# Starting the staging tiles, all slots and the memory's keys at a multiple of 128 bytes

## The chip, the cores and the metric

The kernel runs on one core of a Trainium2 chip. The metric is the device time of one execution in microseconds (us); the time before is the median of three runs. Trace and profile come from one more execution, with the hardware profiler on.

## The reference

One layer of a streaming encoder, all in float32: batch 1, 1024 tokens, width 1024, 256 memory tokens.

```python
h = x
mem_n = rmsnorm(mem, norm_mem_w)
h = h + head_group_mixer(rmsnorm(h, norm_mix_w), ...)           # conv of 31 taps || retention, 8 heads
h = h + memory_cross_attention(rmsnorm(h, norm_xattn_w), mem_n, xq_w, xkv_w, xo_w)   # 4 heads of 256
h = h + sq_relu_mlp(rmsnorm(h, norm_mlp_w), mlp_up_w, mlp_down_w)    # square(relu(h @ up)) @ down, 4096 wide
out = rmsnorm(h, norm_f_w)
```

The mixer projects h to 512 + 512 conv channels, 256 queries, 256 keys, 512 values and 512 gates; one half goes through a gated depthwise convolution, LayerNorm and silu, the other through chunked retention with rotary phases and a GroupNorm; both meet in `w_out`.

## The kernel before, in words

**Products in three parts.** TensorE takes float32 in two formats. Plain float32 serves the transposes and the small products of retention. All large products run in the format fp32r, and to keep precision each operand is split in two tiles, `hi` (rounded to fp32r by ScalarE, line 110) and `lo` (the rest, by VectorE, line 111). `mm3` then issues three matmuls into one PSUM bank: hi x hi (line 128), hi x lo (line 129), lo x hi (line 130). Of each matmul one operand is stationary (128 x 128, loaded ahead by LDWEIGHTS) and one moves through (128 x 512, or 128 x 256 for the memory's projections and the attention scores). In the profile's rows the moving operand is named first, the stationary one second.

**Where tiles lie.** On-chip memory is given out by pools, in bytes of each partition; every tile's size is rounded up to 32 bytes. From the left: `keep` (the identity with the rotary frequencies, 576 bytes; `mhalf`, 8 columns of -0.5 for the power -0.5 in `rstd_of`; `junk`, 4096; `par`, 560), then `raws` (three staging tiles `raw` of 4096, into which weights are loaded), `small` (the `tiny` statistics) and `slots`: 39 tiles `s0` to `s38` of 4096 bytes each. Nearly everything passes through these slots: a free list (`get`, `put`) hands them out and takes them back. The left pools begin at byte 16,512, behind what the runtime and four constants keep.

From the right end of the memory, at byte 229,344, pools come and go by stage: `ra` for retention's small tiles (`qb`, `st`, `rot`, `kT`, ...), `rw` for the residual rows, `rx` for the attention's keys `kT_hi` and `kT_lo` (8192 bytes each), and `rm`, eight more slots `r0` to `r7` for the MLP, which join the free list. When the MLP begins, the three staging tiles join it too.

**Stages in order.** Norm and transposes of memory and x, with the memory's projections in between (0 to 110 us); conv inputs, gates and values, with the 31 taps of each of four channel groups as 124 products on VectorE (line 433; 100 to 295 us); retention and the output projection (to 520 us); cross-attention, and the norm for the MLP (to 690 us); the MLP (690 to 1314 us). The MLP is done as two levels of 2 x 2 blocks with seven products instead of eight, so VectorE also forms sums of weights and of activations (line 907), and results are spilled to DRAM (`a`) and read back.

The order of instructions on each engine is made by the framework's scheduler from its own time model of the program. All DMAs are issued from SP's queue.

Of the kernel before, what the change touches and what calls it, by code (L numbers as in the profile page):

```python
# [7 lines left out]
F32 = mybir.dt.float32  # L8
# [6 lines left out]
P = 128  # L15
# [53 lines left out]
def encoder_layer(ctx: ExitStack, tc: tile.TileContext, x, mem, positions, norm_mix_w, w_in, conv_w, conv_b,  # L69
# [10 lines left out]
    keep = ctx.enter_context(tc.tile_pool(name="keep", bufs=1))  # L80
# [52 lines left out]
    ident_if = keep.tile([P, C_DM], F32, name="ident_if")  # L133
    sync.dma_start(ident_if[:], consts[:, :C_DM])
    ident, invf = ident_if[:, :P], ident_if[:, C_IF:C_DM]
    mhalf = keep.tile([P, 8], F32, name="mhalf")
    vec.memset(mhalf[:], -0.5)

    def rstd_of(ss, n, scale, cols=1):
# [144 lines left out]
    right = ctx.enter_context(ExitStack())  # L284
# [351 lines left out]
    right = ctx.enter_context(ExitStack())  # L636
# [44 lines left out]


    right = ctx.enter_context(ExitStack())
    rx = right.enter_context(tc.tile_pool(name="rx", bufs=1, side="right"))
    kT_hi = rx.tile([P, 8, M], F32R, name="kT_hi")
    kT_lo = rx.tile([P, 8, M], F32R, name="kT_lo")
# [95 lines left out]

    rm = ctx.enter_context(tc.tile_pool(name="rm", bufs=1, side="right"))
    slots.extend(rm, [f"r{i}" for i in range(8)])
    urow = row(norm_mlp_w)
# [413 lines left out]
def build(nc, arrays_of):  # L1201
    args = []
    for name, a in arrays_of:
        args.append(nc.dram_tensor(f"in_{name}_dram", a.shape, mybir.dt.from_np(a.dtype), kind="ExternalInput").ap())
    args.append(nc.dram_tensor("out_0_dram", (1, S, D), F32, kind="ExternalOutput").ap())
    with tile.TileContext(nc, schedule_with_timeline_sim=True) as tc:
        encoder_layer(tc, *args)
# [12 lines left out]
```

## Time and profile before

| | |
|---|---|
| time, median of 3 runs | 1316.72 us (1315.59 to 1317.78) |
| the profiled execution, and its span | 1315.49 us, 1313.7 us |
| TensorE busy, matmuls | 1281.3 us (98%), 6093 |
| VectorE busy | 862.2 us (66%) |
| ScalarE busy | 549.3 us (42%) |
| GpSimd busy | 95.7 us (7%) |
| mean granted TensorE clock | 0.998 of full |
| DMA | 167 MB, queue busy 36.7% of 16 engines |

Matmuls are pipelined: the duration of one in the rows (about 0.39 us for 512 columns) includes its way through the array, while the next one starts some 0.23 us after it. What counts for the pace is the interval between starts, which the timeline gives. A float32 product in the plain format is run as two passes and shows as two matmuls.

### The profile page before, as it was taken

What the parts mean: (1) busy time and instruction counts of PE and PEld (TensorE: products, weight loads), DVE (VectorE), ACT (ScalarE), POOL (GpSimd) and SP (SyncE); (2) the same over time, 40 slices, a digit from 0 to 9 for tenths busy, and PEclk for the clock granted to TensorE, in tenths of its full rate; (3) what the DMA queues carried; (4) which work ended last, traced back from release to release, by engine and by line L of the source; (5) the groups of instructions that cost most, each with busy time, mean ns of one, the idle gap of its engine ahead of it and who ended that gap; (6) DMA issues with size and microseconds to landing.
All of it is one profiled execution on the core that took longest, in us unless ns stands there. A gap on an engine that the chain in (4) does not pass through costs nothing.

```text
span 1313.7 us, 15796 instructions
## 1 busy us (share of the span) xinstructions
PE 1281.3 (98%) x6093; PEld 1061.6 (81%) x6093; DVE 862.2 (66%) x1090; ACT 549.3 (42%) x1015; POOL 95.7 (7%) x157
## 2 busy tenths in 40 slices
PE   6999999999999999999998999999999999999997
PEld 5898887877888888888876888888888888888886
DVE  6676999987756424574568565465565976567744
ACT  7533112155845323452236455444455344323422
POOL 3192000011211000000000000000000000000002
PEclk9999999999999999999999999999999999999999
DMA  9552103312132301322142444333479544444213
GB/s 343 161 155 88 32 17 96 112 41 89 45 132 100 125 0 42 102 98 81 53 140 80 176 176 160 138 103 145 160 272 402 186 148 144 151 147 151 96 64 128
DMA packets 82099, 166.99 MB, mean 127 GB/s; under 512 B 5309, under 2 KB 42309, under 8 KB 82024
## 3 DMA queue, kind: packets, MB, share of 16 engines
q1 hardware_dynamic: 82024, 165.98, 36.7%
q8 instruction: 48, 0.79, 0.2%
q14 instruction: 27, 0.22, 0.1%
HBM read 119.83 MB, written 46.14 MB: 126 GB/s over the span
## 4 chain that ended last, share of the span: by engine, by line
PE 80%; DVE 10%; DMA 4%; POOL 3%; issue 2%; ACT 1%; SPq 0%; POOLq 0%; ACTq 0%; DVEq 0%
PE mm L130 21%; PE mm L129 21%; PE mm L128 21%; DVE s L433 6%; PE tp L129 4%; PE tp L128 4%; PE tp L130 3%; POOL s L328 2%; DVE s L111 2%; POOL s L333 1%; PE mm L516 1%; PE mm L532 1%; DMA s<-in_x_dram 1%; DMA raw<-in_w_out_dram 1%; DMA kvT_d<-s 1%
## 5 line engine op out<-in xcount | busy, mean ns | idle before, releaser
L129 PE MATMUL mm<-s,s 128*128 128x512 f32 (+1 forms) x1298 | 493.6, 381 | 3.9 <-DVE s L111 2.4
L128 PE MATMUL mm<-s,s 128*128 128x512 f32 (+1 forms) x1272 | 484.6, 383 | 3.3 <-ACT s L852 1.0
L130 PE MATMUL mm<-s,s 128*128 128x512 f32 (+1 forms) x1222 | 461.1, 380 | 2.4 <-DVE s L111 2.4
L129 PEld LDWEIGHTS mm<-s,s 128*128 128x128 f32 x1298 | 244.2, 188 | 50.4 <-DVE s L111 3.2
L128 PEld LDWEIGHTS mm<-s,s 128*128 128x128 f32 x1272 | 239.3, 188 | 49.2 <-DVE s L771 1.4
L130 PEld LDWEIGHTS mm<-s,s 128*128 128x128 f32 x1222 | 229.8, 188 | 45.7 <-DVE s L111 3.0
L110 ACT CAST s<-s 128x1024 fp32r<-128x1024 f32 x101 | 104.7, 1050 | 140.7 <-DVE s L907 38.6
L433 DVE SCALAR_TENSOR_TENSOR s<-s,par,s 128x1009 f32<-128x1009 f32 (+25 forms) x120 | 146.2, 1286 | 0.5
L111 DVE TENSOR_TENSOR s<-s,s 128x1024 fp32r<-128x1024 f32 x81 | 98.3, 1223 | 54.6 <-ACT s L110 42.0
L111 DVE TENSOR_TENSOR s<-raw,s 128x1024 fp32r<-128x1024 f32 x64 | 79.1, 1242 | 57.5 <-ACT s L110 23.8
L110 ACT CAST s<-raw 128x1024 fp32r<-128x1024 f32 x66 | 69.2, 1053 | 94.6 <-PE mm L129 15.3
L142 POOL TENSOR_SCALAR tiny<-tiny 128x1 f32<-128x1 f32 (+1 forms) x50 | 17.9, 359 | 1180.2 <-ACT junk L160 925.5
L907 DVE TENSOR_TENSOR s<-s,s 128x1024 f32<-128x1024 f32 x38 | 45.9, 1222 | 7.4 <-DMA s<-in_mlp_down_w_dram 5.3
L129 PE MATMUL mm<-s,r 128*128 128x512 f32 x124 | 48.8, 394 | 0.0
L128 PE MATMUL tp<-s,s 128*128 128x512 f32 x120 | 47.0, 391 | 0.0
L110 ACT CAST s<-r 128x1024 fp32r<-128x1024 f32 x26 | 27.1, 1048 | 42.5 <-PE mm L129 13.5
L130 PE MATMUL tp<-s,s 128*128 128x512 f32 x114 | 44.3, 390 | 0.0
L162 DVE SCALAR_TENSOR_TENSOR s<-s,tiny,s 128x1024 f32<-128x1024 f32 x23 | 29.4, 1283 | 20.2 <-POOL tiny L143 12.8
L111 DVE TENSOR_TENSOR s<-r,s 128x1024 fp32r<-128x1024 f32 x22 | 26.8, 1224 | 22.1 <-ACT s L110 15.5
L130 PE MATMUL mm<-s,r 128*128 128x512 f32 x100 | 39.4, 394 | 0.0
L160 ACT ACTIVATE junk<-s 128x1024 f32<-128x1024 f32 x24 | 25.5, 1064 | 32.8 <-DVE s L1111 24.5
L130 PE MATMUL mm<-r,s 128*128 128x512 f32 x98 | 38.5, 393 | 0.0
(273 smaller groups left out, 1856.1 us busy)
## 6 DMA issues: line engine op xcount, KB each, us to landing
s<-in_mlp_down_w_dram SPq DMA_DIRECT2D x24, 512.0 KB, 3.8
s<-in_mlp_up_w_dram SPq DMA_DIRECT2D x23, 512.0 KB, 4.2
aS<-s SPq DMA_DIRECT2D x22, 512.0 KB, 8.1
raw<-in_w_in_dram SPq DMA_DIRECT2D x20, 512.0 KB, 4.2
s<-aS SPq DMA_DIRECT2D x20, 512.0 KB, 3.3
s<-a SPq DMA_DIRECT2D x19, 512.0 KB, 4.5
a<-s SPq DMA_DIRECT2D x18, 512.0 KB, 2.8
raw<-in_xkv_w_dram SPq DMA_DIRECT2D x16, 512.0 KB, 4.4
```

What stands on the lines that cost most here:

```text
L110: act.copy(hi[:], raw[:])
L111: vec.tensor_tensor(out=lo[:], in0=raw[:], in1=f32(hi[:]), op=ALU.subtract)
L128: pe.matmul(ps, lh, rh, start=first, stop=False, skip_group_check=goes_on)
L129: pe.matmul(ps, lh, rl, start=False, stop=False, skip_group_check=goes_on)
L130: pe.matmul(ps, ll, rh, start=False, stop=last, skip_group_check=goes_on)
L142: pool.tensor_scalar(out=v[:], in0=ss, scalar1=scale, scalar2=EPS, op0=ALU.mult, op1=ALU.add)
L160: act.activation(junk[:], src, AF.Square, accum_out=ss[:])
L162: vec.scalar_tensor_tensor(out=dst, in0=src, scalar=rs[:], in1=r, op0=ALU.mult, op1=ALU.mult)
L328: pool.tensor_scalar(out=o, in0=i, scalar1=a, scalar2=None, op0=op0)
L333: pool.tensor_tensor(out=o, in0=a, in1=b, op=op)
L433: vec.scalar_tensor_tensor(out=accs[m][:, s:], in0=us[m][:, :S - s], scalar=cw(m, k), in1=accs[m][:, s:], op0=ALU.mult, op1=ALU.add)
L907: vec.tensor_tensor(out=o[:], in0=a[:], in1=b[:], op=ALU.subtract)
```

## The change

`mhalf` becomes 32 columns wide (128 bytes instead of 32), which moves everything allocated behind it on the left up by 96 bytes. On the right, a tile of 24 columns (96 bytes) that nobody writes or reads is allocated ahead of the keys' pool `rx` and of the MLP's pool `rm`, which moves their tiles down by 96 bytes. The pools `ra` and `rw` stay where they were.

```diff
-    mhalf = keep.tile([P, 8], F32, name="mhalf")
+    mhalf = keep.tile([P, 32], F32, name="mhalf")
     vec.memset(mhalf[:], -0.5)
...
     right = ctx.enter_context(ExitStack())
+    gap = right.enter_context(tc.tile_pool(name="gapx", bufs=1, side="right"))
+    gap.tile([P, 24], F32, name="rx_gap")
     rx = right.enter_context(tc.tile_pool(name="rx", bufs=1, side="right"))
     kT_hi = rx.tile([P, 8, M], F32R, name="kT_hi")
     kT_lo = rx.tile([P, 8, M], F32R, name="kT_lo")
...
+    gap = ctx.enter_context(tc.tile_pool(name="gap", bufs=1, side="right"))
+    gap.tile([P, 24], F32, name="rm_gap")
     rm = ctx.enter_context(tc.tile_pool(name="rm", bufs=1, side="right"))
     slots.extend(rm, [f"r{i}" for i in range(8)])
```

## The prediction

> **What bounds the kernel now.** I read the page first, then busy time by stretch, then the groups of matmuls by shape, then the timeline of TensorE at six places.
>
> ```profile
> span 1313.7 us, 15796 instructions
> PE 1281.3 (98%) x6093; PEld 1061.6 (81%) x6093; DVE 862.2 (66%) x1090; ACT 549.3 (42%) x1015; POOL 95.7 (7%) x157
> PEclk9999999999999999999999999999999999999999
> PE 80%; DVE 10%; DMA 4%; POOL 3%; issue 2%; ACT 1%; SPq 0%; POOLq 0%; ACTq 0%; DVEq 0%
> ```
>
> TensorE is busy 98% of the span at full granted clock, and 80% of the chain that ended last is TensorE. A change pays here only if it shortens the interval from one matmul to the next, or an idle stretch of TensorE, of which there are 1313.7 - 1281.3 = 32 us. The stretches say where that holds:
>
> ```profile
> core 0: us, PE busy (x) PEld busy (x) DVE busy (x) ACT busy (x) POOL busy (x), PEclk, DMA share, GB/s
> 100.00:295.00 195.00, 190.81 (x853) 155.87 (x852) 177.24 (x184) 49.15 (x118) 10.25 (x18) 1.00 0.21 65
> 295.00:690.00 395.00, 391.88 (x1995) 326.52 (x1994) 223.65 (x431) 170.65 (x499) 29.99 (x60) 1.00 0.25 84
> 690.00:1290.00 600.00, 596.43 (x2593) 487.30 (x2592) 383.74 (x383) 270.90 (x301) 6.17 (x8) 1.00 0.45 161
> ```
>
> In the MLP (690 to 1290 us) VectorE is busy 64% and ScalarE 45%; TensorE alone sets the pace, with 596.4/2593 = 230.0 ns a matmul. In the convolution (100 to 295) VectorE is at 177.2 of 195, so a faster TensorE meets a second bound there after 17.8 us.
>
> **What one matmul costs, and where its operands start.** The starts are not in the trace; they follow from the order and sizes of the tiles. The left pools begin at byte 16,512 = 129 x 128. Ahead of the staging stand 576 + 32 + 4096 + 576 = 5280 = 41 x 128 + 32 bytes, then come 3 x 4096 of staging and 1024 of small tiles: every staging tile and every slot `s` starts 32 bytes past a multiple of 128, and so do all their slices, which are cut at multiples of 512. The right end lies at 229,344 = 1791 x 128 + 96, so the eight slots `r` and the keys start 96 past. No fp32r operand of the kernel starts at a multiple of 128. First both operands at 32 (operands print moving first, stationary second; of each run the first and the last row):
>
> ```profile
> 149.80 0.39 PE L129 MATMUL mm<-s,s 128*128 128x512 f32 x1
> 151.84 0.39 PE L129 MATMUL mm<-s,s 128*128 128x512 f32 x1
> 15.06 0.28 PE L130 MATMUL mm<-s,s 128*128 128x256 f32 x1
> 20.34 0.28 PE L129 MATMUL mm<-s,s 128*128 128x256 f32 x1
> ```
>
> Ten 512-wide matmuls, nine steps: 2.04/9 = 226.7 ns. Forty-five 256-wide ones, 44 steps: 5.28/44 = 120.0 ns. The difference is 106.7 ns for 256 columns, 0.417 ns each, so 512 columns stream in 213.4 ns and 13.3 ns a matmul is something else, the same at both widths: as long as 32 columns, which are 128 bytes of a row. Now plain float32, which the trace runs at half that rate, its operands just as far from a multiple of 128 (96 in `qb`, 32 in `s`):
>
> ```profile
> 301.45 0.59 PE L516 MATMUL mm<-qb,kT 128*128 128x512 f32 x1
> 302.74 0.59 PE L516 MATMUL mm<-qb,kT 128*128 128x512 f32 x1
> 303.17 0.38 PE L524 MATMUL mm<-s,kz 128*128 128x256 f32 x1
> 303.38 0.59 PE L524 MATMUL mm<-s,kz 128*128 128x256 f32 x2
> ```
>
> The first pair is the first and last of four, three steps of 430 ns; the 256-wide take 210 to 220. That is twice the column time and next to nothing beside it: loading a new stationary block costs no 13 ns when the moving operand comes at half rate. The 13.3 ns belongs to reading at full rate. Whether it belongs to the start address, other starts can say:
>
> ```profile
> 1002.76 0.39 PE L128 MATMUL mm<-r,s 128*128 128x512 f32 x1
> 1008.13 0.40 PE L130 MATMUL mm<-r,s 128*128 128x512 f32 x1
> 626.06 0.39 PE L128 MATMUL mm<-s,r 128*128 128x512 f32 x1
> 629.27 0.39 PE L130 MATMUL mm<-s,r 128*128 128x512 f32 x1
> 469.59 0.28 PE L129 MATMUL mm<-kT_lo,s 128*128 128x256 f32 x1
> 470.73 0.28 PE L130 MATMUL mm<-kT_hi,s 128*128 128x256 f32 x1
> ```
>
> Moving at 96, stationary at 32: 24 matmuls, 5.37/23 = 233.5 ns. Moving at 32, stationary at 96: 15 matmuls, 3.21/14 = 229.3 ns. The keys, at 96 and 256 wide: 1.14/10 = 114 ns against 120 at 32. So the interval does hang on where operands start, to a finer or coarser grain than 32 bytes, and not in one direction. No row shows a start at 0; that is the unknown of this change.
>
> **The change, part by part.**
> 1. `mhalf` grows from 8 to 32 columns: staging and all slots `s` move up by 96 bytes, to 21,888 = 171 x 128 and 35,200 = 275 x 128. The gaps on the right move the keys to 212,864 and `r` to 196,480, both multiples of 128. No instruction, DMA or wait is added; the gap tiles are never written. The memset of `mhalf` writes 24 more columns:
>
> ```profile
> L137 DVE MEMSET mhalf<- x1: 65/65/65, 0.8 to 0.8; 128x8 f32 x1
> 1.64 4.51 DMA s<-in_mem_dram
> ```
>
> At VectorE's 1 ns a column or so it goes from 65 to about 90 ns, at 0.8 us, while everything waits for the first load until 6.1 us. Hidden; without that cover 0.03 us.
>
> 2. The interval of the fp32r matmuls. Its price at start 0 is bounded by rows: 213.4 ns (columns alone) from below, 233.5 ns (the dearest start shown) from above. I take 216: the float32 row that streams for the same time, 256 columns at double time, steps at 210 to 220, and it is the nearest row in which TensorE reads without being short of data. The reason for the lower end: the excess is one 128-byte piece at both widths, what a row of 2048 or 1024 bytes costs when it straddles one piece more than it fills (17 instead of 16, 9 instead of 8); from a multiple of 128 it straddles none.
>
> The loops give 4896 fp32r matmuls 512 wide: 2688 in the MLP (8 x 7 x 2 x 4 x 3 up, 2 x 7 x 4 x 4 x 2 x 3 down), 2208 before. MLP: 2688 x (230.0 - 216) = 37.6 us. Before it: 2208 x (226.7 - 216) = 23.6 us. The 576 matmuls 256 wide could give 10 ns each, 5.8 us; but TensorE then also loads a 128-wide block each 109 ns, as the transposes' pace shows:
>
> ```profile
> 20.58 1.47 PE L170 MATMUL tp<-ident_if,s 128*128 128x128 f32 x12
> L170 PE MATMUL tp<-ident_if,s x128: 270/272/273, 20.6 to 468.1; 128*128 128x128 f32 x128
> ```
>
> (1.47 - 0.27)/11 = 109 ns a step. And most of those 576 lie before 110 us among loads and the angle chain. I count 2 of 5.8. Sum before losses: 37.6 + 23.6 + 2 = 63 us.
>
> 3. What is late next. Convolution: some 770 such matmuls give 8.2 us there, out of 17.8 us that VectorE has idle, and its products run back to back:
>
> ```profile
> 174.25 30.83 DVE s L433 x27
> L433 DVE SCALAR_TENSOR_TENSOR s<-s,par,s 128x1009 f32<-128x1009 f32 (+25 forms) x120 | 146.2, 1286 | 0.5
> ```
>
> I give back half, 4 us. Between 295 and 690 us retention, norms and softmax hand over among three engines; of 1995 matmuls' gain I give back 3 us. MLP: splits at 1.05 us on ScalarE and 1.22 on VectorE keep their lead at 64% and 45% busy (68% and 48% after); its DMA share rises from 0.45 to 0.48. I give back 2 us. Sum 63 - 9 = 54 us.
>
> The profiled execution took 1315.5 us (span 1313.7 and 1.8 around it); the median of the runs is 1316.7, 1.2 more. 1315.5 - 54 = 1261.5, as a median 1262.7.
>
> 4. VectorE, ScalarE and DMA read and write the same tiles. The convolution's products already start at every multiple of 4 bytes:
>
> ```profile
> L433 DVE SCALAR_TENSOR_TENSOR s<-s,par,s 128x999 f32<-128x999 f32 x4 | 5.1, 1277 | 0.0
> L433 DVE SCALAR_TENSOR_TENSOR s<-s,par,s 128x1000 f32<-128x1000 f32 x4 | 5.1, 1276 | 0.0
> L433 DVE SCALAR_TENSOR_TENSOR s<-s,par,s 128x1002 f32<-128x1002 f32 x4 | 5.1, 1276 | 0.0
> ```
>
> The output of 1000 columns starts 24 columns in, at 32 + 96 = 128, so at a multiple of 128; its neighbours 4 and 8 bytes away: 1276 to 1277 ns. Nothing for VectorE. For the other two I take nothing: they carry 1% and 4% of the chain, 13 and 53 us, and and a twentieth of these, about the share that the excess has of a matmul, is 0.7 and 2.7 us to either side, within the range below.
>
> [...]
>
> **The rivals.**
> - *Only the mixing goes* (0.27). The excess comes from moving and stationary reads meeting, which hangs on their difference; at 32/32 it is 226.7 and at 0/0 the same. For: the start of the stationary operand shifts the interval too (229.3). Against: the rest is 32 columns to the digit. MLP 2688 x (230.0 - 226.7) = 8.9 us, little elsewhere: about 1308. If the excess falls only in part, to 223 ns (16 columns cheaper from 96 to 32, 8 more from 32 to 0 in proportion to the bytes), 2688 x 7 + 2208 x 3.7 = 27 us: 1290.
> - *Start 0 is a dear one* (0.12), the one on the other side. The keys at 96 are cheaper than 32, `r` at 96 dearer, so the order isn't known. If at 0 both reads begin on the same piece and each matmul takes 233.5 ns, 2688 x 3.5 + 2208 x 6.8 = 24 us slower: 1341. It decides from an interval above some 228.5 ns, the present mean (230.0 MLP, 226.7 before).
> - *The change does nothing* (0.08): no grain that matters, 1316.7; as would a gain that VectorE takes back everywhere, against which stands its 64% in the MLP.
>
> **The numbers.** Forecast, start 0 costs 216 ns: 0.53, with its own range 1250 to 1285 (213.4 ns without losses is 2688 x 16.6 + 2208 x 13.3 = 74 us, 1243; double losses give 1272, 219 ns at that some 1286). The range of 8 in 10 takes in the second case too: 1250 to 1310. A measurement tells 0.2% (2.6 us) from no change. Faster by more: 0.53 + 0.27 = 0.80; within: 0.08; slower: 0.12.
>
> **What would show it.** Steps of 216 ns in the 512-wide runs, the same for `s`, `r` and staging; about 600/217 = 2760 matmuls in 600 us of MLP where 2593 stood; VectorE over 93% in the convolution, with new idle time of TensorE there; float32 steps unchanged at 430 and 215. Wrong if the steps stay at 226.7, or all take one value above 228.5, or if a different order of instructions moves the time more than the steps do (the longer memset enters the scheduler's own time model).

## The result, and the profile after

| | before | changed |
|---|---|---|
| median of 6 runs each | 1317.25 us | 1309.47 us |
| ratio of the changed kernel to before | | 0.9946 (0.9934 to 0.9959) |
| profiled execution, its span | 1315.5 us, 1313.7 us | 1311.6 us, 1309.8 us |

By the medians the change gains 7.8 us (0.59%), by the ratio 0.54%, which is 7.1 us. A gain of 54 us was forecast. It is the first rival, "only the mixing goes", that came out, with its 1308 us. The profiled execution of the changed kernel lies 2.1 us above its median: apart from the very end of the span its granted clock drops to one half in three spells, 13.7 us in all, where the profiled execution before has one spell of 3.4 us. The 512-wide fp32r matmuls that fall into these spells step at 427 ns, which adds 4.2 us to the changed kernel and 1.6 us to the one before. That is one reason why its span shows only half of the gain, 3.9 us; the intervals between matmuls show it better. All ratios in this document leave out two disturbed executions, one of the kernel before (4427 us) and one of e6 (1610 us).

First the page after, with lines that the prediction shows of the page before:

```profile
span 1309.8 us, 15796 instructions
PE 1279.6 (98%) x6093; PEld 1066.4 (81%) x6093; DVE 862.3 (66%) x1090; ACT 548.4 (42%) x1015; POOL 95.7 (7%) x157
PE 78%; DVE 13%; POOL 3%; DMA 3%; issue 2%; ACT 1%; SPq 0%; POOLq 0%; ACTq 0%; DVEq 0%
```

The instructions are the same, each engine is busy for about the same time, and TensorE is still the bound. Busy time by stretch (columns as in the prediction):

```profile
100.00:295.00 195.00, 191.21 (x850) 156.15 (x849) 177.19 (x183) 48.88 (x117) 9.22 (x16) 0.99 0.21 65
295.00:690.00 395.00, 392.10 (x1984) 326.76 (x1983) 223.23 (x430) 169.21 (x497) 29.98 (x60) 1.00 0.26 84
690.00:1290.00 600.00, 596.35 (x2621) 492.73 (x2620) 385.73 (x387) 273.25 (x305) 6.91 (x10) 0.99 0.46 162
```

In the MLP (the last row) 2621 matmuls stand where 2593 stood. That is 596.35/2621 = 227.5 ns a matmul instead of 230.0, and 2688 x 2.5 ns = 6.7 us of the 7.8. The prediction showed a run of 24 matmuls in which `r` moves against `s`; its first and last row are now:

```profile
1002.62 0.39 PE L128 MATMUL mm<-r,s 128*128 128x512 f32 x1
1007.83 0.39 PE L130 MATMUL mm<-r,s 128*128 128x512 f32 x1
```

5.21/23 = 226.5 ns instead of 233.5. But `s` with `s`, now at a multiple of 128 each, has not become faster in itself: in the convolution (100 to 295 us), where both operands lie in `s` throughout, the mean interval of the 512-wide ones is 226.9 ns before and after. Over the whole trace, taking every two 512-wide fp32r matmuls that follow each other within 250 ns, the intervals average 227.1 ns (before 228.6), and 4299 of 4712 are 226 or 227 ns, where 2971 of 4725 were before. The commonest interval is what it was; what went are the longer ones.

### The profile page after: what moved, and what is told of

Read it like the earlier page. It is cut to its first block, busy times and chain, and to the rows that moved or that the text cites. A ratio compares the mean times of both kernels' runs of the same rounds, so it can differ in the third digit from the quotient of the medians.

```text
span 1309.8 us, 15796 instructions
## 1 busy us (share of the span) xinstructions
PE 1279.6 (98%) x6093; PEld 1066.4 (81%) x6093; DVE 862.3 (66%) x1090; ACT 548.4 (42%) x1015; POOL 95.7 (7%) x157
## 4 chain that ended last, share of the span: by engine, by line
PE 78%; DVE 13%; POOL 3%; DMA 3%; issue 2%; ACT 1%; SPq 0%; POOLq 0%; ACTq 0%; DVEq 0%
PE mm L130 21%; PE mm L129 21%; PE mm L128 21%; DVE s L433 9%; PE tp L128 3%; PE tp L130 3%; PE tp L129 3%; DVE s L111 2%; POOL s L328 2%; PE mm L516 1%; POOL s L333 1%; PE mm L532 1%; ACT s L110 1%; DMA raw<-in_w_out_dram 1%; DMA s<-in_conv_w_dram 1%
## 5 line engine op out<-in xcount | busy, mean ns | idle before, releaser
L130 PEld LDWEIGHTS mm<-s,s 128*128 128x128 f32 x1222 | 230.9, 189 | 43.8 <-DVE s L111 1.7
L433 DVE SCALAR_TENSOR_TENSOR s<-s,par,s 128x1009 f32<-128x1009 f32 (+25 forms) x120 | 146.1, 1276 | 0.5
```

Source lines behind the costliest of these rows:

```text
L130: pe.matmul(ps, ll, rh, start=False, stop=last, skip_group_check=goes_on)
L433: vec.scalar_tensor_tensor(out=accs[m][:, s:], in0=us[m][:, :S - s], scalar=cw(m, k), in1=accs[m][:, s:], op0=ALU.mult, op1=ALU.add)
```

## The experiments

There were two theories at first. S: a start at a multiple of 128 pays by itself. D: what counts is how the starts of moving and stationary operand differ. Theory S is the forecast cut down to what the profile had shown.

**Halves of the change, and equal starts at 32.** Either half alone, and a version in which everything starts 32 past a multiple of 128 (the edits in short, against the kernel before):

```diff
 e1_left_only     mhalf 8 -> 32 columns, no gaps
 e2_all_at_32     mhalf 8, both gaps   gap.tile([P, 16], ...)     # 64 bytes
 e3_right_only    mhalf 8, both gaps   gap.tile([P, 24], ...)     # 96 bytes
```

> Only the left half of the change: staging and slots s start at 0 past a multiple of 128, the slots r and the keys stay at 96. Theory D (the interval hangs on the difference between the starts of moving and stationary operand, modulo 128; equal starts give 226.7 ns wherever they lie): s with s steps at 226.7 as before, and runs that mix s and r keep an excess, as the difference is now 96 instead of 64; so the time lies between 0.9946 and 1.003 of before, most likely 0.997 to 1.000. Theory S (a start at a multiple of 128 is what pays, and the profile of the changed kernel shows all that it pays): most fp32r matmuls have both operands in s, so most of the gain comes here, 0.995 to 0.997, and s with s steps differ from those of before.

> The left side as before (32 past a multiple of 128), on the right gaps of 64 bytes, so that r and the keys start at 32 too: all starts alike, none at a multiple of 128. Theory D: the same as the whole change, 0.9935 to 0.996 of before (1309 to 1311 us), mean interval of the 512-wide fp32r matmuls 227.1 ns as there. Theory S: no better than before, 0.998 to 1.002, as nothing starts at a multiple of 128.

> Only the right half: r and the keys at a multiple of 128, staging and slots s at 32 past one. Theory D: the mixed runs have a difference of 32 instead of 64; no gain as with equal starts, 0.996 to 1.003. Theory S: the runs in which r moves (455 matmuls) step at 226.7, a gain of about 2 us, 0.998 to 0.999.

Measured, as ratio to before with the 95% interval: left half 1.0015 (1.0006 to 1.0024), right half 1.0010 (1.0000 to 1.0020), all at 32 0.9999 (0.9990 to 1.0008). Neither half gains, so S falls: most matmuls have both operands in `s`, which the left half alone puts at a multiple of 128. But D modulo 128 falls too: with all starts at 32, the MLP has the old pace.

```profile
690.00:1290.00 600.00, 596.46 (x2593) 488.12 (x2592) 382.49 (x384) 272.08 (x303) 4.52 (x7) 0.99 0.45 160
```

(Busy time by stretch, all starts at 32: 2593 matmuls, as before the change.) What the theory overlooked: in that kernel `s` lies at 288 and `r` at 416 past a multiple of 512, alike modulo 128 and 128 apart modulo 256; in the changed kernel both lie at 384.

**The matmul alone.** A kernel that leaves out the layer and has runs of 48 matmuls, here the loop of one run:

```python
for i in range(REP):      # REP is 48; m, s: first columns of moving and stationary operand, set per run
    a = s + (i % 8) * 128
    b = m + (i % 2) * 512
    pe.matmul(ps[:rows, :cols], st[:, a:a + rows], mv[:, b:b + cols], start=i == 0, stop=i == REP - 1)
```

> The layer is left out; the output is a copy of rows of x. On TensorE stand runs of 48 fp32r matmuls, each with a stationary block of its own (eight in turn) and one of two moving halves, with the starts set: 0/0, 32/32, 64/64, 64/0, 0/64, 96/32, 32/96, 32/0, 0/32, 4/4, 4/0, 96/0, 16/0, 0/96 (moving/stationary, bytes past a multiple of 128); at 0/0 also stationary blocks of 64 and of 32 columns, moving operands of 384 and of 256 columns, and bfloat16. Theory D: 226.7 ns at 0/0, 32/32, 64/64 and 4/4, more (about 233) at differences of 64. Theory S: 0/0 is below 32/32 and 64/64. What the 13.3 ns beyond 512 columns are: if it is the loading of the stationary block that takes reads from the moving operand (theory L), blocks of 64 columns step at about 220 ns and of 32 at about 217, and bfloat16, with half the bytes, at about 216; if it is a fixed cost of each fp32r matmul (theory F), 226.7 for 64 and 32 columns too, and 173.3 for 384 moving columns under both.

In its timeline each run is one row, start and length first. A row ends with its last matmul, so (length - 0.39)/47 is the mean interval of a 512-wide run:

```profile
19.29 11.36 PE L53 MATMUL bboth<-mov,sta 128*128 128x512 f32 x48
41.65 11.36 PE L53 MATMUL dmov<-mov,sta 128*128 128x512 f32 x48
52.84 11.17 PE L53 MATMUL esta<-mov,sta 128*128 128x512 f32 x48
119.83 11.68 PE L53 MATMUL kmovfour<-mov,sta 128*128 128x512 f32 x48
131.35 11.26 PE L53 MATMUL lhalf<-mov,sta 128*64 128x512 f32 x48
142.45 11.23 PE L53 MATMUL mquart<-mov,sta 128*32 128x512 f32 x48
201.25 11.32 PE L53 MATMUL pagain<-mov,sta 128*128 128x512 f32 x48
```

In order, moving/stationary: 32/32 gives 233.4 ns, 64/0 233.4, 0/64 229.4, 4/0 240.2, then 0/0 with stationary blocks of 64 and of 32 columns 231.3 and 230.6, and 0/0 with full blocks 232.6. No 512-wide fp32r run reached 226.7, a miss of both theories as they stood. The short blocks miss both explanations of the 13.3 ns: theory L had them at 220 and 217, theory F at 226.7. The two tiles lay 128 apart modulo 512 here, so equal starts modulo 128 were a difference of 128. That made the theory D256 (or D512): moving and stationary operand must start alike modulo 256 (or 512).

**Deciding on the layer.** Three kernels that differ from the kernel before or from the changed one by the gaps alone, and the change once more (the edits in short):

```diff
 e5_equal_not_128   mhalf 8,  gap.tile([P, 48], ...)   # s, r, keys at 288 modulo 512: alike, none at a multiple of 128
 e6_128_not_equal   mhalf 32, gap.tile([P, 56], ...)   # all at multiples of 128; s at 384, r and keys at 256 modulo 512
 e7_equal_mod_256   mhalf 8,  gap.tile([P, 112], ...)  # s at 288, r and keys at 32 modulo 512
```

> The left side as before, on the right gaps of 192 bytes: staging, slots s, slots r and keys all start at 288 past a multiple of 512, none at a multiple of 128. In the changed kernel all start at 384 past a multiple of 512; in the one with all starts at 32 past a multiple of 128, r lies at 416 and s at 288 past a multiple of 512, which differs by 128. Theory D256/D512 (what counts is that moving and stationary operand start alike modulo 256, or 512): the same gain as the whole change, 0.9935 to 0.996, 512-wide steps 227.1 ns on average. Theory S (multiples of 128): none, 0.998 to 1.002.

> The changed kernel with 128 bytes more in both gaps on the right: every start is a multiple of 128, but r and the keys lie at 256 and s at 384 past a multiple of 512. Theory D256/D512: the gain is gone, 0.998 to 1.002, and r moving against s steps at 231 to 234 ns. Theory S: the gain stays, 0.9935 to 0.996.

> The left side as before, gaps of 448 bytes on the right: s at 288, r and the keys at 32 past a multiple of 512; alike modulo 256, not modulo 512. D256: the gain as in the changed kernel, 0.9935 to 0.996. D512: no gain, 0.998 to 1.002. Theory S: no gain.

> The changed kernel once more beside these on the same chip, for the comparison: 0.993 to 0.996 under every theory.

| | ratio to before | 95% interval |
|---|---|---|
| alike, none at a multiple of 128 (e5) | 0.9943 | 0.9929 to 0.9958 |
| all at multiples of 128, not alike (e6) | 0.9998 | 0.9987 to 1.0010 |
| alike modulo 256 only (e7) | 0.9954 | 0.9940 to 0.9969 |
| the change again (e8) | 0.9942 | 0.9928 to 0.9956 |

The whole gain comes without a single start at a multiple of 128, and with every start at one it is gone. The rows of the MLP for e5, e6 and e7, in this order:

```profile
690.00:1290.00 600.00, 596.36 (x2617) 492.81 (x2616) 385.88 (x387) 272.91 (x304) 6.91 (x10) 0.99 0.46 162
```

```profile
690.00:1290.00 600.00, 596.46 (x2593) 488.02 (x2592) 382.31 (x383) 272.40 (x304) 3.84 (x6) 0.99 0.45 160
```

```profile
690.00:1290.00 600.00, 596.35 (x2622) 492.89 (x2621) 386.50 (x386) 272.82 (x305) 6.66 (x10) 1.00 0.46 163
```

2617, 2593 and 2622 matmuls. In e6 the run of 24 with `r` moving:

```profile
1006.25 0.40 PE L128 MATMUL mm<-r,s 128*128 128x512 f32 x1
1011.62 0.39 PE L130 MATMUL mm<-r,s 128*128 128x512 f32 x1
```

5.37/23 = 233.5 ns, as before the change, from a multiple of 128.

**By difference, alone.** The kernel of e4 with the two tiles alike modulo 512, and moving minus stationary set per run:

> The layer is left out, the output is a copy of rows of x; again runs of 48 fp32r matmuls alone, now by the difference of the starts (moving minus stationary). In the first such kernel the two tiles lay 128 apart modulo 512, so that its runs had differences of 128 (steps 232 to 233 ns), 64 (228.9), 192 (233.3), and never 0. Theory D256/D512: difference 0 gives 226.7 ns wherever the moving operand starts (0, 32, 128 past a multiple of 512; 4 perhaps not), 64 gives 228.9, 192 gives 233.3, 128 gives 232.5. D256: 256 is like 0, 320 like 64, 384 like 128; D512: it isn't. At difference 0, stationary blocks of 64 and 32 columns: theory L (loading them takes the 13.3 ns) 220 and 217 ns; theory F (a fixed cost of an fp32r matmul, whatever it loads) 226.7; 384 moving columns 173.3 under both.

```profile
20.01 11.07 PE L53 MATMUL beq<-mov,sta 128*128 128x512 f32 x48
30.91 11.40 PE L53 MATMUL ceq<-mov,sta 128*128 128x512 f32 x48
42.16 11.07 PE L53 MATMUL deq<-mov,sta 128*128 128x512 f32 x48
53.06 11.36 PE L53 MATMUL eby<-mov,sta 128*128 128x512 f32 x48
64.26 11.37 PE L53 MATMUL fby<-mov,sta 128*128 128x512 f32 x48
86.67 11.32 PE L53 MATMUL hby<-mov,sta 128*128 128x512 f32 x48
97.83 11.36 PE L53 MATMUL iby<-mov,sta 128*128 128x512 f32 x48
109.03 11.05 PE L53 MATMUL jby<-mov,sta 128*128 128x512 f32 x48
119.92 11.16 PE L53 MATMUL kby<-mov,sta 128*128 128x512 f32 x48
153.00 8.48 PE L53 MATMUL nwide<-mov,sta 128*128 128x384 f32 x48
167.07 11.20 PE L53 MATMUL psta<-mov,sta 128*64 128x512 f32 x48
178.10 11.29 PE L53 MATMUL qsta<-mov,sta 128*32 128x512 f32 x48
```

Rows 1 and 3 have difference 0, with both operands moved by 32 and by 128 bytes: 227.2 ns over the whole run, and 226.7 over the last 24 steps. The first 3 to 10 steps of such a run are 224 to 236 ns until the pattern settles. The layer shows the same: in the changed kernel up to 10 steps of 224 to 240 ns follow a break before it is 226 and 227 throughout. Row 2 has difference 0 too, but both operands 4 bytes off: 234.3 ns, as dear as unequal starts. Then come the differences 32 and 64: 233.4 and 233.6; 128: 232.6; 192: 233.4; 256: 226.8, like 0; 320: 229.1. So it is equality modulo 256, between starts that are multiples of 32. That 64 gives 233.6 and 320 gives 229.1, and that 64 gave 229 in e4, are misses of D256 in the dear cases: one difference modulo 256 came out at 229 and at 233.6 ns, and which of the two a run takes isn't explained.

The last two rows, stationary blocks of 64 and of 32 columns at difference 0, stand against theory L: 230.0 and 231.9 ns, not 220 and 217. They miss theory F's 226.7 as well. Loading less is dearer than a full block here (227.2), while at a difference of 128 (e4) it was slightly cheaper, 231.3 and 230.6 against 232.6. Why stays open.

**What is left at difference 0.**

> The layer is left out, the output is a copy of rows of x. What are the 13.3 ns that a fp32r matmul takes beyond its 512 columns when both operands start alike modulo 256? Runs of 48 matmuls at difference 0: six stationary blocks in turn; one stationary block throughout; one moving half throughout; both the same throughout; operands of 64 rows instead of 128; then plain float32 and bfloat16 at differences 0 and 64. Theory F (a fixed cost of an fp32r matmul): 226.7 ns in all fp32r runs. Theory A (the addresses of successive blocks): the runs with one block or one half fall towards 216. Theory R (full-rate reading by all rows): the run of 64 rows falls. Plain float32 has 429 to 430 and bfloat16 216 at both differences, if only reads at the rate of fp32r are sensitive to the starts.

```profile
19.22 11.04 PE L53 MATMUL bone<-mov,sta 128*128 128x512 f32 x48
30.10 11.04 PE L53 MATMUL conemov<-mov,sta 128*128 128x512 f32 x48
41.07 11.19 PE L53 MATMUL dk<-mov,sta 64*128 64x512 f32 x48
52.20 11.17 PE L53 MATMUL eto<-mov,sta 128*128 128x512 f32 x48
63.21 41.36 PE L53 MATMUL ffull<-mvhr,sthr 128*128 128x512 f32 x96
104.41 41.36 PE L53 MATMUL gfull<-mvhr,sthr 128*128 128x512 f32 x96
145.61 10.52 PE L53 MATMUL hbf<-mvb,stb 128*128 128x512 bf16 x48
155.97 10.52 PE L53 MATMUL ibf<-mvb,stb 128*128 128x512 bf16 x48
```

One block throughout and one half throughout: 226.6 ns. Operands of 64 rows and the same pair throughout: 226.7 over the last 24 steps (their rows are longer by a break and a slow start, 229.8 and 229.4 ns over the whole run; six blocks in turn, once more at the end, took 11.24 us, 230.9 ns over the whole run). Theories A and R fall. Of the theories, F fits best for full blocks: 512 columns and 13.3 ns. What the 13.3 ns are, no run shows: every one of these matmuls loads its block again, also in the run with one block throughout (its trace has 48 loads; in the layer, where lines 128 and 129 share a block, 6093 matmuls have 6093), so a fixed cost of the load itself isn't ruled out. Plain float32 at differences 0 and 64 has the same 41.36 us, start to start 429 ns, two of them a product; bfloat16 the same 10.52 us, start to start 215.8 ns. Of the three formats only fp32r depends on the starts, as far as these two differences tell, and only it has the 13 ns: bfloat16's 215.8 and plain float32's 429 ns stand beside 213.4 and twice 213.4.

## Why the prediction was wrong

- **The bound** held: TensorE is 98% busy, and the time moved with the interval of its matmuls alone.
- **The step that failed is the price in part 2**: "I take 216", with the reason that the excess is one 128-byte piece that a misplaced row straddles. At multiples of 128 the interval is 226.7 ns still, the mean of the 512-wide ones in the MLP of the changed kernel (e4: 232.6 there, where the two starts differ by 128 modulo 256). In e9, with both operands moved from 32 to 128 bytes behind the start of their tiles, it stays at 226.7 (rows of 11.07 us both), so no straddled piece is in it. The 13.3 ns, 32 columns "to the digit", come with every fp32r matmul at its best: 384 columns from equal starts step at 173.3 ns over the last 24, which is 160.0 and 13.3 again (the row above: 8.48 us). A number that fits a mechanism to the digit was taken for the mechanism. The widths could not tell one more piece from a constant; only other starts could.
- **What the rows did say was read half**: 233.5 and 229.3 ns showed that both starts matter, the stationary one too. That speaks for a relation between the two reads, and no row showed a full-rate matmul at 216. It was put at 0.27 as "hangs on their difference", and priced nearly right: 8.9 us in the MLP against 6.7 measured, 1308 against 1309.5. That 1309.5 lies just inside the wide range of 1250 to 1310 is due to this rival, for which the range was stretched; the forecast's own range ended at 1285.
- **That the change gained at all is luck.** It was made for starts at multiples of 128. That it also put `s` and `r` alike, both at 384 modulo 512, was not aimed at: e6 has every start at a multiple of 128 as well, and gains nothing.
- The part by which it would have given 223 ns (in proportion to the bytes) did not come either: the commonest interval stayed at 226 to 227.
- **Start 0 is a dear one** did not come: of the starts at a multiple of 32 that ran with equal ones, none is dear in itself (0, 32 and 128 in e9, 227.0 to 227.2 ns over the run; 288 in e5 and 384 in the changed kernel, 226.5 with `r` moving). The decision point was well placed: the mean went from 228.6 to 227.1.
- **The keys**, which were to be moved with the rest, step at 120 ns in the changed kernel (119.7 on average), where they stepped at 113 to 119 before (117.5; difference 192): 192 matmuls, some 0.4 us lost. For 256-wide matmuls equal starts are not the cheapest: alone, they step at 120.0 ns at difference 0 (e9, a row of 5.91 us) and at 118.6 at 128 (e4, 5.86 us).
- **VectorE and the memset**: nothing, as said (the memset takes 85 ns instead of 65, about 90 were estimated). In the convolution VectorE is busy 177.2 of 195 us before and after, and the products take what they took:

```profile
L433 DVE SCALAR_TENSOR_TENSOR s<-s,par,s 128x1009 f32<-128x1009 f32 (+25 forms) x120 | 146.1, 1276 | 0.5
```

They take 146.1 us in all, 146.2 before. The mean of one went from 1286 to 1276 ns, and it is 1262 in e5, where `s` lies as before, so that isn't the start. The order of instructions did not change on any engine, so the scheduler has no part in it. What part 3 gave back to VectorE, ScalarE and DMA was not put to the test, as TensorE hardly got faster.
- **The change does nothing** did not come either: the starts are not alike, 226.7 against 233.4 ns between starts that are all multiples of 32 (e9).
- **The formats.** bfloat16 and plain float32 take 215.8 and 429 ns at both differences that were run (e10). For fp32r the interval hangs on where the stationary block lies relative to the moving operand (233.5 ns in e6 against 226.5 in the changed kernel, with the same instructions). That the two reads get in each other's way is the obvious reading of this, but no run shows the meeting itself.

## What to carry to other kernels

For fp32r matmuls 384 or 512 columns wide, place moving and stationary operands at multiples of 32 bytes so that their starts agree modulo 256 bytes. Where the tiles come from several pools, check the pools' starts against each other, not against a round number. It is worth up to 3% of each matmul that has it wrong (233.4 against 226.7 ns at 512 columns; at 384, 175.8 in e4 against 173.3 in e9, rows of 8.61 and 8.48 us); here, before the change, 37% of the 512-wide intervals lay off 226 to 227 ns. Before a constant is booked as recoverable, find one row that runs without it under the same format, or measure it alone.

## What the runs showed of the hardware that was not expected

- An fp32r matmul of 256, 384 or 512 columns takes its columns at 0.417 ns and 13.3 ns more (120.0, 173.3, 226.7 ns from equal starts, e9; the 512-wide one also with one stationary block, 226.6, or eight, and with 64 or 128 rows, e10); bfloat16 takes 215.8 ns for 512.
- At 512 columns that best interval is reached only with starts equal modulo 256 bytes, and only after the first steps of a run (224 to 236 ns). The other differences at multiples of 16 bytes that were run come out at 229 to 234 ns; with an operand 4 bytes off it is 234 to 240, even where both are off alike (234.3, e9, row 2).
- From equal starts a shorter stationary block makes it dearer, not cheaper: 230.0 ns with 64 columns, 231.9 with 32, against 227.2 with 128 (whole runs, e9). At a difference of 128 it makes it slightly cheaper, 231.3 and 230.6 against 232.6 (e4). Not explained.
